# Seven block products for the up projection in half of each MLP

## The chip, the cores and the metric

The kernel runs on one core of one Trainium2 chip. The metric is the device time of one execution in microseconds: before the change the median of three runs is 1108.54, from 1107.82 to 1109.71.

TensorE (PE in the profile) multiplies matrices into PSUM, VectorE (DVE), ScalarE (ACT) and GpSimd (POOL) work on elements, SyncE (SP) issues transfers. Each engine runs its own instructions strictly in the order written for it and waits for the others by semaphores.

## The reference, cut to what matters

A two-layer encoder steps over 512 prompt tokens and 64 sampled ones, all in float32, 1024 wide. Layer 0 mixes tokens by causal pooling, layer 1 by sparse attention (an indexer picks keys, then grouped attention with rotary). Each layer ends with an MLP of hidden width 4096, and a last norm closes the step:

```
def _mlp(h, w_up, w_down):
    u = jax.nn.relu(h @ w_up)
    return (u * u) @ w_down

x = x + y                                        # y: the mixer's output
x = x + _mlp(_rmsnorm(x, norm_mlp[i]), mlp_w_up[i], mlp_w_down[i])
```

The change is in the two MLPs alone: 576 tokens x 1024 x 4096, up and down, in each layer.

## The kernel before

**Precision.** A float32 operand is held as two reduced parts: a high part wh or uh, made by a cast on ACT (L189, `wh`), and the rest wl or ul, made by a subtract on DVE (L190, `wl`). A product is three matmuls, wh by uh, wh by ul and wl by uh. A weight "unit" is 128x512 elements in both parts, and there are six plus two unit buffers in an MLP.

**Tokens and quarters.** The 576 tokens lie in columns, in two halves of 288. The hidden width is done in four quarters (c = 0 to 3) of 8 blocks of 128 rows. For each quarter, first up: a block takes two units and 48 matmuls (8 input tiles x 3 x 2 halves) into a double PSUM bank `up`, of which there are two. Then relu times the norm's scale on DVE (L385), the square on ACT (L386).

**Down by seven products.** Down takes rows and tokens in pairs. Over 2x2 blocks, b11 to b22 of activations, Strassen's scheme with Winograd's sums needs seven block products in place of eight. `factors` (L398 on) makes the operands: three blocks of the activations (L402 and L408, high and low part) and the four sums t1 to t4 (L403 to L406, then L407 and L409) into the tile u; the sums of weights come from two accumulating DMAs and two POOL adds (L231, L237). For each pair q of output blocks the three banks a, b and c take the products: b11 into a, t2 into b, t1 into c, then b21 into a, t3 into b, b22 into c, t4 into b, 84 matmuls in all. The first product b11 is needed in three outputs; it is collected over the quarters in a sum g on DVE (L476) and added to the residual x by three POOL operations at the last quarter (L481 to L483).

**The order.** A tile scheduler decides the order on each engine from priorities and free buffers before the program runs; the order is then fixed. In the program text, the first block of the next quarter's up stands ahead of each down, so that PE has work while the operands of down are made.

**Loads.** Weights come from memory in blocks of 128x1024; SP issues them into two plus two raw buffers. In the second layer's last quarter, two output blocks are left to the plain products of `last`, which also ends the kernel with the final norm; the tiles `rest` hold the block of activations that u lacks for it.

Of the kernel before, what the change touches and what calls it, by code (L numbers as in the profile page):

```python
# [43 lines left out]
UNITS = (6, 2)  # L44
# [3 lines left out]
RAWS = (2, 2)  # L48
MLP_BLOCKS = ("up", "even", "odd", "down")
LOADS_AHEAD = {True: 3, False: 1}  # L50
UP_ORDER = (0, 4, 1, 5, 2, 6, 3, 7)
FACTORS = ("b11", "b22", "b21", "t1", "t2", "t3", "t4")
# [3 lines left out]
def pool_dsa_kernel(ctx: ExitStack, tc: tile.TileContext, a, o):  # L56
# [5 lines left out]
    weights = ctx.enter_context(tc.tile_pool(name="weights", bufs=UNITS[0]))  # L62
# [73 lines left out]
    turns = {"raw": 0, "unit": 0, "spare": 0}  # L136

    def longer(what, sizes, mlp):

        if not (mlp and "more" in phase):  # L140
            return False
        t, turns[what] = turns[what], turns[what] + 1
        return t * sizes[1] // sum(sizes) != (t + 1) * sizes[1] // sum(sizes)

    def raw_tile(mlp=False):
        pool = phase["more"] if longer("raw", RAWS, mlp) else raws
        return pool.tile([P, 4 * 264], F32, tag="raw", name=uid("raw"))

    def load(src, n, queue, mlp=False):
        raw = raw_tile(mlp)  # L150
        queue.dma_start(raw[:, :n], src)
        return raw
# [3 lines left out]
    def mlp_jobs(layer, plain=0):  # L156
        for c in range(4):
            ups = [("up", a["w_up"][layer, c * 8 + f], KT * P) for f in UP_ORDER]
            jobs.extend(ups[1:] if c else ups)
            if c < 3:  # L160
                jobs.append(("up", a["w_up"][layer, (c + 1) * 8 + UP_ORDER[0]], KT * P))
# [14 lines left out]
    def unit(n=512, mlp=False):  # L176

        pool = phase["more"] if longer("unit", UNITS, mlp) else weights
        return [pool.tile([P, 528], F32R, tag=t, name=uid(t))[:, :n] for t in ("wh", "wl")]
# [7 lines left out]
    def split_unit(src, mlp, spare=False):  # L187
        h, l = spare_unit() if spare else unit(src.shape[1], mlp)
        act.copy(h, src)  # L189
        how["sub"].tensor_tensor(l, src, f32(h), ALU.subtract)  # L190
        return h, l

    def loaded():

        waiting = []
        while jobs or waiting:
            while jobs and len(waiting) < LOADS_AHEAD["more" in phase]:
                kind, src, n = jobs.pop(0)
                mlp = kind in MLP_BLOCKS
                raw = load(src, n, nc.sync if mlp else act, mlp)[:, :n]  # L200
                sums = None
# [167 lines left out]
    def mlp(layer, gi, late=0, end=None):  # L369
# [5 lines left out]
        def pairs(c):  # L375

            return (KT - LAST if end and c == 3 else KT) // 2
# [1017 lines left out]
```

## Time and profile before

| what | value |
|---|---|
| median of three runs | 1108.54 us |
| the profiled execution | 1109.8 us |
| its span in the profile | 1108.0 us |
| PE busy | 1087.8 us, 98% of the span |
| DVE busy | 821.8 us, 74% |
| ACT busy | 540.2 us, 49% |
| POOL busy | 348.6 us, 31% |
| moved by DMA | 138.73 MB, 125 GB/s |

The profiled execution lies 1.3 us above the median, and 1.8 us of it lie outside its span. A row of the page names the line of the kernel, the engine, the operation, and the tiles it writes and reads. The rows that start with a time are single instructions, or runs of them in the chain of waits: start, length, engine, and in brackets how long the engine had been idle and which instruction ended the wait. The span starts with the pool mixer; the first MLP lies from about 41 to 428 us, attention from 428 to about 706, the second MLP then to about 1083.

### The profile page before, as it was taken

What the parts mean: (1) busy time and instruction counts of PE and PEld (TensorE: products, weight loads), DVE (VectorE), ACT (ScalarE), POOL (GpSimd) and SP (SyncE); (2) the same over time, 40 slices, a digit from 0 to 9 for tenths busy, and PEclk for the clock granted to TensorE, in tenths of its full rate; (3) what the DMA queues carried; (4) which work ended last, traced back from release to release, by engine and by line L of the source; (5) the groups of instructions that cost most, each with busy time, mean ns of one, the idle gap of its engine ahead of it and who ended that gap; (6) DMA issues with size and microseconds to landing.
All of it is one profiled execution on the core that took longest, in us unless ns stands there. A gap on an engine that the chain in (4) does not pass through costs nothing.

```text
span 1108.0 us, 21062 instructions
## 1 busy us (share of the span) xinstructions
PE 1087.8 (98%) x8222; PEld 1066.4 (96%) x8222; DVE 821.8 (74%) x1502; ACT 540.2 (49%) x969; POOL 348.6 (31%) x325
## 2 busy tenths in 40 slices
PE   9999999999999999999889999999999999999997
PEld 8999999999999999999888898999999999999996
DVE  7867856866786797779987944767756866786784
ACT  8545434434434545344367776545434434434542
POOL 3312201302221261227686893012211302231241
PEclk9999999999999999999988999999999999999999
DMA  6443543554364345457741444543543554355212
GB/s 220 138 105 77 161 134 82 118 162 115 87 161 130 90 115 174 120 158 186 200 110 49 136 138 143 166 106 77 161 134 79 123 161 115 86 162 131 68 42 86
DMA packets 60611, 138.73 MB, mean 125 GB/s; under 512 B 9969, under 2 KB 21536, under 8 KB 60512
## 3 DMA queue, kind: packets, MB, share of 16 engines
q1 hardware_dynamic: 46544, 103.50, 30.9%
q0 software_dynamic: 8928, 16.26, 9.4%
q10 hardware_dynamic: 5040, 17.63, 5.1%
q8 instruction: 65, 1.06, 0.4%
q14 instruction: 34, 0.28, 0.1%
HBM read 122.28 MB, written 10.89 MB: 120 GB/s over the span
## 4 chain that ended last, share of the span: by engine, by line
PE 82%; DVE 5%; DMA 4%; SPq 2%; POOL 2%; issue 2%; ACT 2%; ACTq 0%; DVEq 0%; POOLq 0%
PE up L277 37%; PE b L445 13%; PE c L445 8%; PE a L445 8%; PE wo L277 3%; PE sc L1092 2%; PE pj L277 2%; PE wa L277 2%; PE pt L1118 1%; PE pb L826 1%; DMA raw<-in_w_in 1%; PE dn L277 1%; PE o L1150 1%; PE o L1143 1%; SPq L1265 1%
## 5 line engine op out<-in xcount | busy, mean ns | idle before, releaser
L277 PE MATMUL up<-xs,wh 128*128 128x288 f32 x2048 | 356.7, 296 | 0.2
L189 ACT CAST wh<-raw 128x512 fp32r<-128x512 f32 (+1 forms) x316 | 194.4, 621 | 306.2 <-PE up L277 133.0
L277 PEld LDWEIGHTS up<-xs,wh 128*128 128x128 f32 x2048 | 300.3, 188 | 1.0 <-DVE v L385 0.6
L190 DVE TENSOR_TENSOR wl<-raw,wh 128x512 fp32r<-128x512 f32 (+1 forms) x292 | 236.4, 813 | 63.2 <-ACT wh L189 57.9
L277 PE MATMUL up<-xs,wl 128*128 128x288 f32 x1024 | 219.2, 295 | 0.0
L277 PEld LDWEIGHTS up<-xs,wl 128*128 128x128 f32 x1024 | 164.4, 188 | 0.1
L445 PE MATMUL b<-u,wh 128*128 128x288 f32 x744 | 150.6, 296 | 0.2 <-DVE x L490 0.2
L231 POOL TENSOR_TENSOR sum<-sum,raw 128x512 f32<-128x512 f32 x31 | 52.7, 1701 | 243.7 <-DMA raw<-in_w_down 196.4
L445 PEld LDWEIGHTS b<-u,wh 128*128 128x128 f32 x744 | 119.5, 188 | 0.6 <-DVE x L490 0.4
L445 PE MATMUL b<-u,wl 128*128 128x288 f32 x372 | 109.4, 296 | 0.0
L189 ACT CAST wh<-sum 128x512 fp32r<-128x512 f32 x93 | 56.9, 620 | 107.6 <-PE up L277 42.9
L445 PE MATMUL a<-u,wh 128*128 128x288 f32 x496 | 101.5, 295 | 0.0
L445 PE MATMUL c<-u,wh 128*128 128x288 f32 x496 | 100.8, 295 | 0.0
L385 DVE SCALAR_TENSOR_TENSOR v<-up,rbm 128x576 f32<-128x576 f32 x60 | 45.2, 756 | 67.8 <-PE up L277 63.1
L214 POOL DMA_DIRECT2D raw<-in_w_down x31 | 27.0, 871 | 186.2 <-DMA raw<-in_w_down 93.1
L190 DVE TENSOR_TENSOR wl<-sum,wh 128x512 fp32r<-128x512 f32 x93 | 78.6, 849 | 3.8 <-ACT wh L189 2.5
L445 PEld LDWEIGHTS a<-u,wh 128*128 128x128 f32 x496 | 79.9, 188 | 0.0
L445 PEld LDWEIGHTS c<-u,wh 128*128 128x128 f32 x496 | 79.6, 188 | 0.1
L445 PE MATMUL a<-u,wl 128*128 128x288 f32 x248 | 73.5, 296 | 0.1
L445 PE MATMUL c<-u,wl 128*128 128x288 f32 x248 | 73.3, 295 | 0.0
L445 PEld LDWEIGHTS b<-u,wl 128*128 128x128 f32 x372 | 69.9, 188 | 0.0
L213 POOL DMA_DIRECT2D sum<-in_w_down x31 | 28.1, 915 | 125.2 <-DVE wl L190 86.7
(256 smaller groups left out, 2015.5 us busy)
## 6 DMA issues: line engine op xcount, KB each, us to landing
raw<-in_w_up SPq DMA_DIRECT2D x64, 512.0 KB, 3.6
raw<-in_w_down SPq DMA_DIRECT2D x64, 512.0 KB, 3.6
raw<-in_w_o ACTq DMA_DIRECT2D x16, 512.0 KB, 3.9
sum<-in_w_down SPq DMA_DIRECT2D x31, 256.0 KB, 3.8
sum<-in_w_down POOLq DMA_DIRECT2D x31, 256.0 KB, 5.3
raw<-in_w_down POOLq DMA_DIRECT2D x31, 256.0 KB, 4.1
raw<-in_w_in ACTq DMA_DIRECT2D x15, 512.0 KB, 4.4
q<-st SPq DMA_DIRECT2D x32, 144.0 KB, 2.5
```

The source lines that it names most:

```text
L189: act.copy(h, src)
L190: how["sub"].tensor_tensor(l, src, f32(h), ALU.subtract)
L213: pool.dma_start(s1, odd[:, 512:], accum_op=ALU.add)
L214: pool.dma_start(raw[:, :512], even[:, :512], accum_op=ALU.add)
L231: pool.tensor_tensor(s2, s1, a11, ALU.add)
L277: pe.matmul(pt[h][:, :m] if isinstance(pt, tuple) else pt[:, h, :m], wt, xs[k][:, part, c:c + m], start=(k == 0 and i == 0), stop=(k == n ...
L385: dve.scalar_tensor_tensor(v, pt[:, :, :HT], 0.0, halves(norm.rb), ALU.max, ALU.mult)
L445: pe.matmul(bank[:, :HT], wt, ut, start=first and j == 0 and i == 0, stop=last and j == 3 and i == 2, skip_group_check=True)
L826: pe.matmul(pt[:, c0:c0 + rhs.shape[1]], lhs, rhs, start=n == 0, stop=n == len(steps) - 1)
L1092: pe.matmul(pt[:, hh, :nw], q[:, 2 * s + hh], ks[g][:, part, :nw], start=part == 0, stop=part == 1)
L1118: pe.transpose(pp[:, c:c + P], pr[:, hh, kt * P:(kt + 1) * P], ident)
L1143: pe.matmul(oc[:, 2 * s + hh], pT[:, c:c + P], V[:, kt, vs], start=kt == 0, stop=kt == i)
```

## The change

Quarters 0 and 1 of each MLP (`PLAIN_CHUNKS = 2`) keep the plain up projection. In quarters 2 and 3 up is done by the same seven products as down: `seven` serves both, with the class `Up` or `Down` for what is done with the banks. For up the operands are halves of the normed x: four blocks are views of the tiles xs, the sums t1, t2 and t4 are made in quarter 0 from x (`x_sums`, between blocks three to six, three DVE operations, one ACT cast and one DVE subtract for each of four tiles `xt`), and t3 by a change of xs in place at the end of quarter 1 (`x_difference`).

The order of products is another: b11 goes into bank b, and ACT copies bank b into bank a (L511). Then t1 into c, t2 on top of b, b21 on top of a, t3 onto b, b22 onto c, t4 onto b. So the first product reaches all three outputs in PSUM, and neither g nor the POOL operations at the end are left. In the first four such groups of an MLP one extra matmul writes bank a ahead of the copy (L510, `SEEDED`). No block of the next quarter stands ahead of down any more. The raw buffers and the loads are halves of a block, four plus three; six units serve everything, the buffers of sums are three in place of four.

```diff
-FACTORS = ("b11", "b22", "b21", "t1", "t2", "t3", "t4")
+PLAIN_CHUNKS = 2
+SEEDED = 4
+FACTORS = ("t3", "t1", "t2", "b11", "b22", "b21", "t4")
...
+        def x_sums(j):
+            t = x_sums_tile()
+            xt.append(t)
+            raw, first = rough[:, 3 * j:3 * j + 3], rough[:, 12 + j % 2]
+            gain, minus = gv[:, gi, j:j + 1], negative[:, half + j:half + j + 1]
+            act.activation(first, x[j][:, :HT], AF.Copy, scale=gain)
+            dve.scalar_tensor_tensor(raw[:, 0], x[j][:, HT:], gain, first, ALU.mult, ALU.subtract)
+            dve.scalar_tensor_tensor(raw[:, 1], x[half + j][:, :HT], minus, raw[:, 0], ALU.mult, ALU.subtract)
+            dve.scalar_tensor_tensor(raw[:, 2], x[half + j][:, HT:], minus, raw[:, 1], ALU.mult, ALU.subtract)
+            act.copy(t[:, :, 0], raw)
+            dve.tensor_tensor(t[:, :, 1], raw, f32(t[:, :, 0]), ALU.subtract)
...
+        def seven(operand, late, on):
+            b, a_, c = (psum1(t) for t in "bac")
+            on.banks = [t[:, :HT] for t in (a_, b, c)]
+            w = next_unit()
+            product(b, w, operand, "b11", rows, True)
+            tasks[0] += 1
+            if tasks[0] <= SEEDED:
+                pe.matmul(a_[:, :HT], w[0][:, :P], operand(0, "b11", 0), start=True, stop=True, skip_group_check=True)
+            act.copy(a_[:, :HT], b[:, :HT])
+            w1 = next_unit()
+            if late:
...
+            else:
+                product(c, w1, operand, "t1", rows, True)
+                on.c()
+                product(b, next_unit(), operand, "t2", rows)
+            on.b()
+            for bank, factor, then in ((a_, "b21", on.lo0), (b, "t3", on.hi1), (c, "b22", on.hi0), (b, "t4", on.lo1)):
+                product(bank, next_unit(), operand, factor, rows)
+                then()
...
+            def hi0(self):
+                v = self.v
+                dve.tensor_tensor(v[:, 0], self.banks[2], snap[:, 1], ALU.add)
+                self.relu(0, v[:, 0], ALU.max, 0)
+                if end and self.at[0] == 3:
+                    left_over(self.at[1], v[:, 0])
+                first_sum(v)
+                middle_sums(v)
+                parts_of(self.u, v, slice(0, 3))
+
+            def lo1(self):
+                v = self.v
+                self.relu(5, self.banks[1], ALU.min, 1)
+                last_sum(v)
+                parts_of(self.u, v, slice(5, 7))
...
-        steps = [s for c in range(4) for s in [(c, i) for i in range(c > 0, 8)] + ([(c + 1, 0)] if c < 3 else []) + [(c, None)]]
...
+            if c < PLAIN_CHUNKS:
...
+                    if c == 0 and 2 <= i < 6:
+                        x_sums(i - 2)
+                if c == PLAIN_CHUNKS - 1:
+                    snap = halves(tmp("snap", "s2", 1))
+                    for j in range(half):
+                        x_difference(j)
+            else:
+                for j in range(half):
+                    up = Up(c, j)
+                    seven(of_x, False, up)
+                    us.append(up.u)
+            for q in range(pairs(c)):
+                seven(of(us), q == 0, Down(q))
```

Three places of the order, where rows read: line, operation, tile written, tiles read, shape.

First, ACT in quarter 0 of the first MLP, around the up blocks six and seven (casts of weights `wh`, of sums of x `xt`, of operands of down `u`, and squares of `v`). Before:

```order
L189 CAST wh_182_1165<-raw_162_1018 128x512
L189 CAST wh_184_1169<-sum_181_1163 128x512
L386 ACTIVATE v_161_1015<-v_161_1015 128x576
L402 CAST u_169_1080<-v_161_1015 128x3x288
L189 CAST wh_189_1234<-sum_171_1091 128x512
L407 CAST u_169_1080<-t_168_1079 128x4x288
```

Now:

```order
L181 CAST wh_188_1152<-sum_162_924 128x512
L434 CAST xt_183_1137<-rough_126_686 128x3x288
L472 CAST u_154_901<-v_153_900 128x7x288
L455 ACTIVATE v_172_1053<-v_172_1053 128x2x288
L455 ACTIVATE v_172_1053<-v_172_1053 128x576
```

and DVE at the same place, now:

```order
L182 TENSOR_TENSOR wl_189_1153<-sum_162_924,wh_188_1152 128x512
L435 TENSOR_TENSOR xt_183_1137<-rough_126_686,xt_183_1137 128x3x288
L473 TENSOR_TENSOR u_154_901<-v_153_900,u_154_901 128x7x288
L463 SCALAR_TENSOR_TENSOR v_172_1053<-up_171_1004,rbm0_148_863 128x2x288
L463 SCALAR_TENSOR_TENSOR v_172_1053<-up_182_1080,rbm0_148_863 128x576
```

The casts of u were two of three and four pieces behind squares; now one of seven pieces stands behind a cast of xt, and the relu of bank up_171 stands behind its subtract.

Second, DVE where the third quarter goes from up to down. Before:

```order
L385 SCALAR_TENSOR_TENSOR v_469_3284<-up_478_3305,rbm0_140_841 128x576
L190 TENSOR_TENSOR wl_493_3435<-sum_473_3295,wh_492_3434 128x512
L404 TENSOR_TENSOR t_479_3356<-v_469_3284,t_479_3356 128x288
L405 TENSOR_TENSOR t_479_3356<-v_469_3284 128x288
L406 TENSOR_TENSOR t_479_3356<-v_469_3284,t_479_3356 128x288
L408 TENSOR_TENSOR u_480_3357<-v_469_3284,u_480_3357 128x3x288
L190 TENSOR_TENSOR wl_495_3439<-raw_462_3221,wh_494_3438 128x512
L409 TENSOR_TENSOR u_480_3357<-t_479_3356,u_480_3357 128x4x288
L385 SCALAR_TENSOR_TENSOR v_486_3423<-up_485_3374,rbm0_140_841 128x576
```

Now:

```order
L479 SCALAR_TENSOR_TENSOR v_523_3407<-v_523_3407 128x288
L480 TENSOR_TENSOR v_523_3407<-v_523_3407 128x288
L565 SCALAR_TENSOR_TENSOR v_523_3407<-b_525_3409,rbm0_148_863 128x288
L473 TENSOR_TENSOR u_524_3408<-v_523_3407,u_524_3408 128x2x288
L182 TENSOR_TENSOR wl_555_3585<-sum_537_3471,wh_554_3584 128x512
L473 TENSOR_TENSOR u_524_3408<-v_523_3407,u_524_3408 128x3x288
L483 SCALAR_TENSOR_TENSOR v_523_3407<-v_523_3407 128x288
L182 TENSOR_TENSOR wl_557_3589<-raw_515_3322,wh_556_3588 128x512
L473 TENSOR_TENSOR u_524_3408<-v_523_3407,u_524_3408 128x2x288
```

The parts of the last operands u_480 stood ahead of the next quarter's block up_485; those of u_524 stand behind the relu of bank b_525, the last product of up.

Third, PE at the same place. Before, the end of the next quarter's block, then down:

```order
L277 MATMUL up_485_3374<-xs_117_653,wh_466_3231 128x288 x4
L277 MATMUL up_485_3374<-xs_117_653,wl_467_3232 128x288 x2
L445 MATMUL a_487_3426<-u_431_2946,wh_474_3297 128x288 x2
L445 MATMUL a_487_3426<-u_431_2946,wl_475_3298 128x288
L445 MATMUL a_487_3426<-u_446_3079,wh_474_3297 128x288 x2
```

Now, the end of the last up group (t4 into b_525) with down's b11 around it:

```order
L496 MATMUL b_548_3562<-u_499_3253,wh_538_3473 128x288 x2
L496 MATMUL b_548_3562<-u_499_3253,wl_539_3474 128x288
L496 MATMUL b_525_3409<-xt_155_905,wh_533_3448 128x288 x2
L496 MATMUL b_525_3409<-xt_155_905,wl_534_3449 128x288
...
L496 MATMUL b_525_3409<-xt_183_1137,wl_534_3449 128x288
L496 MATMUL b_548_3562<-u_524_3408,wh_538_3473 128x288 x2
L496 MATMUL b_548_3562<-u_524_3408,wl_539_3474 128x288
L496 MATMUL c_550_3564<-u_449_2943,wh_541_3493 128x288 x2
```

Three of the four parts of down's first product moved ahead of t4; the fourth, of u_524, follows t4 at once.

More of the change, by code (lines that the diff above doesn't have):

```diff
@@ L43 @@
 HEADS = {"a": 512, "c": 1024, "d": 1024}
-UNITS = (6, 2)
+UNITS = 6
 UNDER = 64
@@ L134, in __getitem__, with raw_tile, load @@
             return self.t[k // 2][:, k % 2]
[L136 to L152, printed above, removed]
+    turns = {"spare": 0}
+    def raw_tile(pool=raws, n=2 * 264):
+        return pool.tile([P, n], F32, tag="raw", name=uid("raw"))
+    def load(src, n, queue):
+        halves = [raw_tile()[:, :n // 2] for _ in range(2)]
+        for i, raw in enumerate(halves):
+            queue.dma_start(raw, src[:, i * n // 2:(i + 1) * n // 2])
+        return halves
     jobs = []
@@ L369, in mlp, with x_sums_tile, room @@
     def mlp(layer, gi, late=0, end=None):
-        norm = Norm(f"m{layer}")
-        xs = split_x(gi, norm, lambda k: pair_slot("xs", "xs"), late)
-        part_sums = [None] * (KT // 2)
-        rest = [None] * 4
+        scratch = []
+        def x_sums_tile():
+            return phase["xt"].tile([P, 3, 2, HT], F32R, tag="xt", bufs=KT // 2, name=uid("xt"))
+        def room():
+            if not scratch:
+                t = f32(x_sums_tile())
+                scratch.extend(t[:, i].rearrange("p a t -> p (a t)") for i in range(3))
+            return scratch.pop(0)
@@ L440, in product, with tiles, parts_of, first_sum @@
-        def product(bank, w, us, factor, js, first, last):
+            square(v)
+        def tiles():
+            return (phase["acts"].tile([P, 7, HT], F32, tag="v", bufs=1, name=uid("v")),
+                    phase["u"].tile([P, 7, 2, HT], F32R, tag="u", bufs=4, name=uid("u")))
+        def parts_of(u, v, f):
+            act.copy(u[:, f, 0], v[:, f])
+            dve.tensor_tensor(u[:, f, 1], v[:, f], f32(u[:, f, 0]), ALU.subtract)
+        def first_sum(v):
+            dve.tensor_tensor(v[:, 1], v[:, 3], v[:, 0], ALU.subtract)
@@ L441, in product @@
             for j in js:
                 wh, wl = (t[:, j * P:(j + 1) * P] for t in w)
-                uh, ul = (us[j][:, FACTORS.index(factor), i] for i in range(2))
+                uh, ul = (operand(j, factor, part) for part in range(2))
                 for i, (wt, ut) in enumerate(((wh, uh), (wh, ul), (wl, uh))):
-                    pe.matmul(bank[:, :HT], wt, ut, start=first and j == 0 and i == 0, stop=last and j == 3 and i == 2,
+                    pe.matmul(bank[:, :HT], wt, ut, start=first and j == 0 and i == 0, stop=j == 3 and i == 2,
@@ L545, in last @@
+        if end:
+            rest = []
+            for j in range(half):
+                if j % 2 == 0:
+                    t = x_sums_tile()
+                rest.append(t[:, j % 2])
+                split(rest[j], parked[j // 2][:, j % 2, :HT])
+            b11, b22, b21 = ([u[:, FACTORS.index(f)] for u in us] for f in ("b11", "b22", "b21"))
+            end([rest + b22, b11 + b21])
     def last(parts):
```

348 lines of the change are left out of this document (185 added, 163 removed).

## The prediction

> **What bounds the kernel now.** I read the totals and the groups of the page first, then the chain, the stages, and single instructions.
>
> ```profile
> PE 1087.8 (98%) x8222; PEld 1066.4 (96%) x8222; DVE 821.8 (74%) x1502; ACT 540.2 (49%) x969; POOL 348.6 (31%) x325
> L277 PE MATMUL up<-xs,wh 128*128 128x288 f32 x2048 | 356.7, 296 | 0.2
> L277 PE MATMUL up<-xs,wl 128*128 128x288 f32 x1024 | 219.2, 295 | 0.0
> ```
>
> PE has work 98% of the span; the up projections of both layers are 2048 + 1024 = 3072 of its 8222 matmuls. The 295 ns of one is not its cost, since matmuls overlap. The cost is read from the chain of waits, in order of time, where runs of matmuls have a length and a count:
>
> ```profile
> 62.36 0.77 DVE v L385
> 63.13 0.04 issue
> 63.17 38.52 PE up L277 x288
> ...
> 205.31 1.59 PE b L445 x12
> ...
> 243.52 49.45 PE up L277 x372
> ```
>
> 49.45 / 372 = 0.1329 us for one matmul of 288 columns; a product of down (12 matmuls) takes 1.59 us, the same rate. An up block of 48 is 6.4 us. So from 63.17, where the fourth block of the first quarter starts, blocks end at about 69.6, 76.0 and 82.4.
>
> ```profile
> core 0: us, PE busy (x) PEld busy (x) DVE busy (x) ACT busy (x) POOL busy (x), PEclk, DMA share, GB/s
> 42.00:102.00 60.00, 59.92 (x447) 59.26 (x447) 42.47 (x69) 29.08 (x44) 8.87 (x7) 1.00 0.36 87
> 146.00:201.00 55.00, 55.00 (x416) 55.00 (x415) 34.39 (x50) 24.05 (x33) 9.58 (x8) 1.00 0.40 106
> 201.00:242.00 41.00, 41.00 (x311) 41.00 (x310) 33.64 (x54) 16.47 (x27) 9.47 (x8) 1.00 0.57 145
> 428.00:676.00 248.00, 238.38 (x1874) 223.50 (x1873) 194.20 (x499) 142.52 (x341) 150.98 (x148) 0.97 0.48 137
> 1083.00:1108.00 25.00, 17.41 (x130) 16.22 (x129) 11.04 (x32) 5.49 (x13) 3.12 (x4) 0.94 0.29 95
> ```
>
> These stages are the first quarter's up, the third quarter's up and down, attention, and the end. PE is full in every MLP stage. DVE is full to 34.39/55 = 63% in a plain up stage, but to 33.64/41 = 82% in a seven-product stage: seven products put more on DVE for less on PE. This is what the change does to up.
>
> **What the change removes.** In quarters three and four of both layers the up projection falls from 8 x 48 = 384 matmuls to 4 x 84 = 336. That is 48 x 4 = 192 fewer, at 0.1329 us: **-25.5 us**. PE is full there, so the whole of it is gain unless something else becomes late. The rest of the sum is what becomes late.
>
> **Seeds.** The first four seven-product groups of each MLP issue one more matmul (L510): 8 x 0.133 = **+1.1**. The copies of bank b into bank a (L511, ACT) lie beside three later products (t1, t2: 3.2 us) before b21 needs bank a; ACT is busy 16.47 of 41 us there. Nothing. The sums g that they replace (L476 on DVE, three POOL adds at the end) free time on engines with room; nothing either.
>
> **The first quarter.** The sums of x for the later quarters are made between blocks three to six. On ACT (first order listing) the cast of wh_188 waits for a unit that the sixth block still reads, until 82.4. Behind it on ACT stand a cast of an x sum and the 7x288 cast of u_154, on DVE the subtract of u_154, and behind that (DVE row `L463 ... up_171_1004`) the relu that frees the double bank into which the seventh block writes; there are two such banks, used in turn. PE waits for this chain. Its durations:
>
> ```profile
> 82.38 0.62 ACT L189 CAST wh<-sum 128x512 fp32r<-128x512 f32 x1 [2.62 <-PE up L277]
> ...
> 153.53 0.69 ACT L386 ACTIVATE v<-v 128x576 f32<-128x576 f32 x1 [0.43 <-DVE v L385]
> 154.25 0.92 ACT L402 CAST u<-v 128x864 fp32r<-128x864 f32 x1
> ...
> 156.19 1.16 ACT L407 CAST u<-t 128x1152 fp32r<-128x1152 f32 x1
> ```
>
> ```profile
> 152.73 0.76 DVE L385 SCALAR_TENSOR_TENSOR v<-up,rbm 128x576 f32<-128x576 f32 x1 [2.09 <-PE up L277]
> ...
> 154.62 0.45 DVE L405 TENSOR_TENSOR t<-v 128x288 f32<-128x288 f32 x1
> 154.99 0.45 DVE L406 TENSOR_TENSOR t<-v,t 128x288 f32<-128x288 f32 x1
> 155.36 1.05 DVE L408 TENSOR_TENSOR u<-v,u 128x864 fp32r<-128x864 f32 x1
> 156.33 0.68 DVE L190 TENSOR_TENSOR wl<-raw,wh 128x512 fp32r<-128x512 f32 x1
> ```
>
> ```profile
> 87.88 1.35 DVE L409 TENSOR_TENSOR u<-t,u 128x1152 fp32r<-128x1152 f32 x1
> 89.15 0.75 DVE L385 SCALAR_TENSOR_TENSOR v<-up,rbm 128x576 f32<-128x576 f32 x1
> ```
>
> From start to start DVE takes 0.37 us for 288 elements (154.62 to 154.99), 0.97 for 864 (155.36 to 156.33) and 1.27 for 1152 (87.88 to 89.15): 0.30 per further 288, so 0.67 for 576 and 2.17 for 2016. ACT needs 0.92 and 1.16, so 1.88 for 2016. The chain: 82.4 + 0.62 (wh_188) + 0.92 (x sum, 864) + 1.88 (u_154) + 2.17 (its subtract) + 0.76 (relu) = 88.8. PE meanwhile has 13 matmuls of down ahead of the seventh block, 1.7 us. The stall is 6.4 - 1.7 = 4.7 us: 6.5 if two POOL adds (0.9 each, below) delay DVE inside it, and 0 if the order of the engines bends so that the relu is done before, which a fixed order excludes. The second layer has the same order: **+9.3** for both. In the old order a cast and a square stand there, and each double bank is read out one block after it was filled.
>
> **From up to down.** Before, the first up block of the next quarter (6.4 us of PE) ran between the last finished up block and down; now nothing does. Down's first product is drawn into the last up group by the scheduler for three of its four factors (third listing), but its last part, and the next product after, read u_524's b11, whose subtract (second order listing, `L473` into u_524, 128x2x288) stands behind the relu of bank b (`L565 ... b_525`), which waits for the last matmul of t4. So PE waits a relu of 288 (0.45 by the 288 rows), the subtract of 576 (0.75) and handovers of about 0.05 to 0.1: 1.1 to 1.7. Four such places: **+5.2**. Before, the same relu had a block to hide behind. The second quarter hands over to down with a plain block's relu (0.76), square (0.69 for 576 elements, as ACT L386 below), two sums (0.74), a cast (0.62, by 512) and a subtract (0.68), 3.5 us, while down has 33 matmuls, 4.4 us, that do not need it: covered by 0.9. For slips there, and for the last group of each MLP, whose t4 follows t3 in the same bank after an update (0.45), **+1.0**, between 0 and 4 x 0.9.
>
> **DVE in the up groups.** One up group asks of DVE seven weight splits (0.60 from start to start, 208.28 to 208.88 below), ten operations of 288 (0.37), and part subtracts of 576, 864 and 576 (0.67, 0.97 and 0.67): 4.2 + 3.7 + 2.3 = 10.2 us, against 84 x 0.1329 = 11.2 us of PE. That would fit, but POOL's two adds for each group stop some of it:
>
> ```profile
> 202.72 0.45 DVE L478 TENSOR_TENSOR x<-x,c 128x288 f32<-128x288 f32 x1
> 203.09 1.64 DVE L190 TENSOR_TENSOR wl<-sum,wh 128x512 fp32r<-128x512 f32 x1
> 204.65 0.68 DVE L190 TENSOR_TENSOR wl<-raw,wh 128x512 fp32r<-128x512 f32 x1
> 205.25 0.44 DVE L476 TENSOR_TENSOR g<-g,a 128x288 f32<-128x288 f32 x1
> ...
> 208.28 0.68 DVE L190 TENSOR_TENSOR wl<-raw,wh 128x512 fp32r<-128x512 f32 x1
> 208.88 0.44 DVE L490 TENSOR_TENSOR x<-x,c 128x288 f32<-128x288 f32 x1
> ```
>
> ```profile
> 202.89 1.29 POOL L237 TENSOR_TENSOR sum<-sum,raw 128x512 f32<-128x512 f32 x1 [2.04 <-DVE wl L190]
> ```
>
> ```profile
> L190 DVE TENSOR_TENSOR wl<-raw,wh 128x512 fp32r<-128x512 f32 x18 | 16.0, 887 | 0.9
> L190 DVE TENSOR_TENSOR wl<-sum,wh 128x512 fp32r<-128x512 f32 x9 | 7.0, 793 | 0.2
> ```
>
> ```profile
> L237 POOL TENSOR_TENSOR sum<-sum,raw 128x512 f32<-128x512 f32 x3 | 4.5, 1502 | 2.0 <-DVE wl L190 2.0
> L231 POOL TENSOR_TENSOR sum<-sum,raw 128x512 f32<-128x512 f32 x2 | 3.0, 1479 | 3.1 <-DVE wl L190 3.1
> ```
>
> While POOL adds from 202.89 to 204.18, a split that takes 0.68 elsewhere takes 1.64; the updates of x that read PSUM keep their 0.45. In 201 to 242 the 27 splits took 23.0 us, 4.6 over 27 x 0.68, for five POOL adds: 0.9 us each. The Trainium skill, "GPSIMD Engine Reference", Specifications, says that GpSimd shares its SBUF interfaces with VectorE and contends with DVE instructions that have two SBUF inputs; the trace agrees, 1.64 against 0.68.
>
> With two adds a group costs DVE 10.2 + 1.8 = 12.0 us, 0.8 more than PE. DVE falls behind; what it owes is paid where PE waits for DVE in earnest, at the relu of bank b ahead of down. Of the last group's work 3.9 us stand behind that relu (three part subtracts 2.3, one operation of 288, two splits of 0.6): 48.0 - 3.9 = 44.1 us of DVE ahead of it against 44.6 of PE in a stage of four groups. That leaves no debt, if DVE never idles in between; it does where it waits for a square or a cast, by a few tenths each time. I take one group's excess, 0.9 a stage, between 0 and the whole 3.4: four stages, **+3.6**. Inside the stage a debt of that size is covered: splits are made up to five products (5 x 1.59 us) ahead of use. In down a group asks DVE for 4.2 + 6 x 0.37 = 6.4 us and two adds: room.
>
> **The clock.** In the stages where PE has idle time its granted clock is 0.97 and 0.94, elsewhere 1.00. The new stalls of the first quarter come in pieces (to the u_154 cast, to its subtract, to the relu) of 2.4, 1.8 and 0.3 us, by the chain above; were the clock 0.94 over such a stall's 25 us, as at the end, a layer would lose 1.5. I take **+0.8** for both, 0 to 3.0. The Trainium skill, "TensorE: Matmul & The Clock Gate", HAM oscillation, speaks against the change here: an idle gap of over about 3.4 us sends the array back to half clock for some microseconds, which I estimate by that page at 1.7 us lost each time; by it the term is 0 if the gaps stay in pieces and 3.4 if they join. No run here shows it yet in an MLP stage.
>
> **The sum.** -25.5 + 1.1 + 9.3 + 5.2 + 1.0 + 3.6 + 0.8 = -4.5 us. The profiled execution took 1109.8 (span 1108.0 and 1.8 around it), 1.3 over the median of 1108.54; 1109.8 - 4.5 = 1105.3, and on the basis of the median **1104.0**.
>
> **The rivals.**
>
> 1. *The stalls hide.* If DVE keeps up in the up groups and the chain of the first quarter is not on PE's path (the relu before the big subtract, or down's products long enough to cover it), the seeds and half of the transitions remain: -25.5 + 1.1 + 2.6 = -21.8, **1086.7**. For it: ACT and DVE are busy 29.08 and 42.47 of the 60 us there, so what holds PE up is order, not load. Against: that order is fixed, and each link's duration is measured.
>
> 2. *DVE bounds the up groups: slower.* The place is the third and fourth quarters' up, the mechanism the stretched splits above with more weight: an up group has eight DVE operations with two SBUF operands beside its seven splits, where a down group has the splits alone, so an add can stop DVE for its whole 1.5 us. Then a group is 10.2 + 2 x 1.5 = 13.2 us, a stage 52.8 - 3.9 = 48.9 against PE's 44.6: 4.3 of debt at the relu ahead of down, four times 17.2 in place of 3.6. 1104.0 + 13.6 = **1117.6**. It decides from a debt of 0.9 + 4.5 / 4 = 2.0 a stage on, which is 12.6 us a group; there the gain is gone. For it: DVE is at 82% in down already. Against: the excess measured is 0.9 an add, not 1.5.
>
> 3. *Loads come late.* Seven half blocks are held where four whole ones were, and the sums, made of two transfers in turn, have three buffers for four. If this costs PE 1 us in each of the 16 up groups, 1104 + 16 = **1120**. Against: PE is full in every MLP row above, with the DMA share at 0.36 to 0.57.
>
> **How the numbers follow.** My forecast (1098 to 1110) has 0.45, rival 1 and what lies toward it (1084 to 1098) 0.25, rival 2 with what lies toward it (1110 to 1122) 0.23, rival 3 0.07. What a measurement of this kernel can tell from no change is about 0.2%, 2.2 us: 1106.3 to 1110.8 is the same. Of my forecast's 0.45 some 0.27 lies below 1106.3, with 0.25 from rival 1: faster 0.52. 0.16 of the forecast and 0.01 of rival 2 lie within: same 0.17. The rest, 0.02 of the forecast, 0.22 and 0.07, is slower: 0.31. The range leaves out a third of rival 1's side and, above, rival 3 and the top of rival 2, about 0.1 each: 1088 to 1118; the forecast's own is 1098 to 1110.
>
> **What would show it.** In the changed profile: PE's idle time in the up stage of the first quarter, put down to DVE's relu of the up tile, near 4.7 us and twice; four waits of 1.1 to 1.7 us for the tile u ahead of down's second product; in a stage of up groups a DVE share of nine tenths or more and at its end about 1 us more of that wait; copies into bank a with nothing waiting; 1536 matmuls into tile up in place of 3072, at 0.133 us each. I am wrong if up groups take over 12.5 us each, if PE waits for weights (wl, DVE) all along, or if the first quarter shows no stall.

## The result and the profile after

The changed kernel takes 1120.24 us (median of 4 runs, 1118.69 to 1125.15) against 1109.12 for the kernel before on the same occasions: 1.0109 times as long, 95% interval 1.0075 to 1.0142. It is slower by 11 us. The forecast was 1104.0 with a range of 1088 to 1118.

The profiled execution (span 1116.8) has the matmuls that were promised and does not turn them into time. Page and list of waits of PE (us in total, times, longest) of the changed kernel:

```profile
PE 1070.4 (96%) x8038; PEld 1040.5 (93%) x8038; DVE 889.0 (80%) x1655; ACT 607.4 (54%) x1152; POOL 389.1 (35%) x363
...
L496 PE MATMUL b<-u,wh 128*128 128x288 f32 x992 | 205.0, 298 | 15.9 <-DVE u L473 7.9
```

```profile
PE b L496 <- DVE v L579: 8.2, 12, 1.1
PE b L496 <- DVE u L473: 7.9, 6, 2.0
PE b L496 <- ACT u L472: 5.8, 6, 1.7
PE b L496 <- DVE x L536: 2.0, 3, 1.4
```

PE issues 184 matmuls fewer and is busy 17 us less, while DVE is busy 67 us more. PE's four longest sums of waits are all for one bank, b, 18.1 of the 23.9 us for DVE and the rest for ACT: L579 is the add that reads bank b after t3, ahead of t4; L472 and L473 make the operands u of down. The wait rows fall short by some 0.16 us each, since a matmul's modelled end (295 ns behind its start) lies behind the start of the next (133 ns).

By stages, core 0, the columns being length, busy time and instructions of PE, weight loads, DVE, ACT and POOL, the granted clock, DMA share and GB/s. Before, the first quarter's up and the third quarter's up:

```profile
41.34:101.53 60.19, 60.11 (x450) 59.45 (x448) 42.85 (x69) 29.27 (x45) 9.46 (x8) 1.00 0.36 86
243.35:292.81 49.46, 49.46 (x375) 49.46 (x373) 32.55 (x47) 22.81 (x32) 9.18 (x7) 1.00 0.35 93
```

After, the first quarter's up, the third and fourth quarter's up, and the same of the second MLP:

```profile
41.58:103.41 61.83, 57.57 (x415) 56.02 (x414) 47.00 (x79) 31.22 (x49) 5.18 (x5) 0.97 0.28 72
...
246.16:293.20 47.04, 45.19 (x335) 44.02 (x334) 44.16 (x75) 32.51 (x64) 18.55 (x16) 1.00 0.66 156
...
339.42:387.31 47.89, 44.94 (x336) 44.02 (x334) 44.95 (x75) 32.35 (x64) 18.24 (x16) 1.00 0.64 154
...
706.58:768.72 62.14, 58.35 (x414) 56.76 (x412) 41.85 (x72) 28.56 (x43) 5.15 (x5) 0.95 0.31 84
909.96:957.44 47.48, 45.08 (x335) 44.15 (x334) 44.49 (x75) 32.34 (x64) 18.25 (x16) 1.00 0.66 158
1003.68:1052.10 48.42, 44.95 (x336) 44.01 (x334) 45.63 (x79) 35.20 (x72) 18.62 (x16) 1.00 0.66 159
```

A stage of up groups is 333 matmuls, 44.3 us at 0.1329. It takes 47.0 to 48.4, and DVE is busy 44 to 46 of them: 94%. The first quarter has PE idle and a clock below 1.00 in both layers.

If each stage's length is set against its count of matmuls at 0.1329 us, the difference of 8.7 us between the two spans (1116.8 and 1108.0, rounded) is made up like this, in us for both layers:

| place | forecast | profiled |
|---|---|---|
| 184 matmuls fewer (192 less 8 seeds) | -24.4 | -24.5 |
| first quarter's up: stall and half clock | +10.1 | +12.9 |
| third and fourth quarter's up: waits inside and at its end | +3.6 | +13.8 |
| down behind them: rest of the way in, half clock, updates | +5.2 | +8.4 |
| down of quarters one and two, up of quarter two | +1.0 | +2.8 |
| all outside the two MLPs | 0 | -4.8 |

### The profile page after: what moved, and what is told of

Read it like the earlier page. It is cut to its first block, busy times and chain, and to the rows that moved or that the text cites. A ratio compares the mean times of both kernels' runs of the same rounds, so it can differ in the third digit from the quotient of the medians.

```text
span 1116.8 us, 21753 instructions
## 1 busy us (share of the span) xinstructions
PE 1070.4 (96%) x8038; PEld 1040.5 (93%) x8038; DVE 889.0 (80%) x1655; ACT 607.4 (54%) x1152; POOL 389.1 (35%) x363
## 4 chain that ended last, share of the span: by engine, by line
PE 72%; DVE 17%; issue 4%; DMA 3%; ACT 1%; POOL 1%; SPq 0%; DVEq 0%; ACTq 0%; POOLq 0%
PE b L496 21%; PE up L305 17%; PE c L496 11%; PE a L496 5%; DVE wl L182 4%; PE pj L305 3%; DVE u L473 3%; PE wo L305 3%; PE wa L305 2%; PE sc L1219 2%; PE pt L1245 2%; DVE v L565 1%; PE v L1119 1%; DVE work L1172 1%; PE pb L953 1%
## 5 line engine op out<-in xcount | busy, mean ns | idle before, releaser
L496 PE MATMUL b<-u,wh 128*128 128x288 f32 x992 | 205.0, 298 | 15.9 <-DVE u L473 7.9
L305 PE MATMUL up<-xs,wh 128*128 128x288 f32 x1024 | 180.0, 298 | 1.0 <-DVE v L463 1.0
L305 PEld LDWEIGHTS up<-xs,wh 128*128 128x128 f32 x1024 | 151.4, 190 | 1.9 <-DVE v L463 1.5
L260 POOL TENSOR_TENSOR sum<-sum,raw 128x512 f32<-128x512 f32 x47 | 74.6, 1588 | 220.4 <-DMA raw<-in_w_down 127.6
L182 DVE TENSOR_TENSOR wl<-sum,wh 128x512 fp32r<-128x512 f32 x141 | 96.5, 685 | 25.5 <-ACT wh L181 22.1
L305 PE MATMUL up<-xs,wl 128*128 128x288 f32 x512 | 110.0, 296 | 0.0
L473 DVE TENSOR_TENSOR u<-v,u 128x576 fp32r<-128x576 f32 (+3 forms) x76 | 85.8, 1129 | 15.8 <-ACT u L472 15.3
L264 POOL TENSOR_TENSOR sum<-sum,raw 128x512 f32<-128x512 f32 x47 | 72.6, 1545 | 48.5 <-DVE wl L182 34.7
L305 PEld LDWEIGHTS up<-xs,wl 128*128 128x128 f32 x512 | 82.9, 190 | 0.0
L472 ACT CAST u<-v 128x576 fp32r<-128x576 f32 (+3 forms) x76 | 68.6, 902 | 24.3 <-DVE v L483 15.2
L455 ACT ACTIVATE v<-v 128x288 f32<-128x288 f32 (+1 forms) x96 | 49.9, 523 | 36.7 <-DVE v L565 21.7
L305 PE MATMUL pj<-xs,wh 128*128 128x288 f32 x352 | 62.0, 295 | 1.3 <-ACT xs L294 1.3
```

What stands on the lines that cost most here:

```text
L260: pool.tensor_tensor(s2, s1, a11, ALU.add)
L264: pool.tensor_tensor(s2, s2, a12, ALU.add)
L305: pe.matmul(pt[h][:, :m] if isinstance(pt, tuple) else pt[:, h, :m], wt, xs[k][:, part, c:c + m], start=(k == 0 and i == 0), stop=(k == n ...
L455: act.activation(v, v, AF.Square)
L472: act.copy(u[:, f, 0], v[:, f])
L473: dve.tensor_tensor(u[:, f, 1], v[:, f], f32(u[:, f, 0]), ALU.subtract)
```

## The experiments

All runs are compared with runs of the kernel before on the same chip (median 1110 to 1111 us); the ratio is to those. Where a run is set against the changed kernel, the difference is that of the two medians; the changed kernel ran beside a median of 1109.1, so by the ratios every run below stands 1 to 3.5 us better against it. The names of lines move by a few where an edit adds lines.

**The two halves of the change apart.**

```diff
-PLAIN_CHUNKS = 2
+PLAIN_CHUNKS = 4
```

with the sums of x gone and the leftover operand split where its block is finished.

> All four quarters keep the plain up projection, and the sums of x are gone; down has the new order of products with the copy of the first product within PSUM, the half-block loads and the six units of the changed kernel. It parts the two halves of the change. Theory (the loss lies in the up groups and in the sums of x): seeds 1.1 us, 0 to 0.9 us at each of eight ways from up to down, and if the 4.5 us that attention gained in the changed kernel come from its loads they show here too: 1105 to 1113 us. Rival (the new down costs by itself, by copies in PSUM or late loads): 1116 or more.

Measured: 1111.29 us, ratio 1.0019 (0.9996 to 1.0043). The new down, its copies in PSUM and the half loads cost nothing that these runs tell from zero (the interval reaches to 4.8 us), and gain nothing. In the profiled executions the two MLPs and the end take 1.6 us more than before, attention 2.4 less. The loss, but for that, belongs to the seven products of up and their sums of x. The first quarter's up, without sums:

```profile
41.53:95.81 54.28, 54.19 (x409) 53.54 (x407) 36.95 (x60) 25.29 (x41) 5.56 (x5) 1.00 0.32 82
```

**The sums of x.**

```diff
                         if i:
                             norm.stats()
+                            x_sums(0)
+                            x_sums(1)
                         continue
+                    if c == 0 and i == 2:
+                        x_sums(2)
...
-                    if c == 0 and 2 <= i < 6:
-                        x_sums(i - 2)
+                    if c == 0 and i == 2:
+                        x_sums(3)
```

> The changed kernel, with the sums of x made in blocks two and three of the first quarter, where DVE is idle for 12 of 18 us, in place of blocks three to six. Theory (the two stalls ahead of the seventh block, 4.1 us each, come of the queue of sums, casts and the 7x288 subtract, and the half clock that follows costs another 1.7 and 3.4): all of it goes, 1120.2 - 13 = 1107 us. Rival (DVE is overloaded in that quarter anyway, so the stall comes one block later): 1117 to 1121.

Measured: 1113.76 us, ratio 1.0029 (1.0015 to 1.0044), 6.5 us less than the changed kernel: half of the theory. First quarters of this run:

```profile
41.93:101.82 59.89, 56.08 (x409) 54.89 (x408) 46.51 (x79) 30.55 (x49) 5.56 (x5) 0.97 0.28 75
705.94:760.70 54.76, 54.26 (x407) 53.61 (x406) 41.90 (x72) 27.44 (x43) 5.55 (x5) 1.00 0.35 95
```

In the second layer the stall and the half clock are gone, 62.14 us to 54.76 (6 of the 397 matmuls of up and early down now lie in the next stage, 0.8 us). In the first layer DVE is still busy with the norm at that time, and the sums now delay it: PE waits 2.7 us for the norm's sums and 1.6 for the next relu.

**POOL's adds.**

```diff
-            s2 = phase["sums"].tile([P, 512], F32, tag="sum", name=uid("sum"))
-            pool.tensor_tensor(s2, s1, a11, ALU.add)
+            s2 = s1
...
-                if n == 3:
-                    pool.tensor_tensor(s2, s2, a12, ALU.add)
```

> The changed kernel with POOL's two adds for each seven-product group left out; the sum that they made is replaced by another tile, so the products with it have other values. Theory (t4 waits for an add on DVE that is late because splits are stretched while POOL adds): without them DVE needs 10.2 us for an up group of 11.2, the waits of t4 fall from 10.4 us to the 0.35 that t3 right ahead of t4 costs in any case, 16 times: 5 us less, and the waits of down for DVE's updates go, 2 more: 1112 to 1114 us. Rival (the waits come of t4 standing right behind t3 alone): 1118 to 1120.

Measured: 1103.50 us, ratio 0.9937 (0.9917 to 0.9957): 16.7 us less than the changed kernel, more than twice the theory's 7. The third and fourth quarter's up of this run:

```profile
245.36:289.81 44.45, 44.12 (x336) 43.88 (x334) 39.79 (x75) 31.87 (x64) 6.90 (x8) 1.00 0.68 166
335.90:380.37 44.47, 44.12 (x335) 43.89 (x333) 39.81 (x75) 31.87 (x64) 6.90 (x8) 1.00 0.70 165
```

The same 75 operations of DVE take 39.8 us in place of 44.2 and 45.0, the same 333 matmuls 44.45 in place of 47.0 and 47.9, and no wait of t4 is left in the list of waits. So the place of t4 behind t3 costs nothing by itself (the rival), and the four stages give 11.7 of the 15.5 us between the two profiled executions. The run leaves out two things at once: the stretch of DVE's operations, and the wait of ACT's casts for POOL's sums (15.6 us of ACT's idle time in the changed kernel). The rows show the first, on the engine that t4 waits for; what the second is worth was not parted from it.

**The order of the last products.**

```diff
+                if factor == "b22":
+                    with tc.issue_after(third):
+                        product(bank, next_unit(), operand, factor, rows)
```

where `third` is the last matmul of t3.

> The changed kernel with the order of PE held as the program text has it: t3, then b22, then t4, in place of b22, t3, t4. Theory (t4 waits for the add that reads bank b after t3; 1.6 us of b22 between them cover the add's 0.45 and up to 1.1 of lateness): the waits of t4 fall from 10.4 us to 0 to 2 us, 1110 to 1112 us. Rival (DVE is the bound of the up groups, 12 us against 11.2, so the debt is only paid later, at the way into down): 1117 to 1120.

Measured: 1127.59 us, ratio 1.0156 (1.0123 to 1.0189): 7 us slower than the changed kernel by the medians and 5 by the ratios, whose intervals overlap: that it gains nothing is sure, that it loses is not. The add that t4 waits for is line 585 here:

```profile
PE b L496 <- DVE u L473: 9.2, 6, 2.1
PE b L496 <- ACT u L472: 5.7, 4, 1.8
PE b L496 <- DVE v L585: 4.7, 4, 1.6
PE b L496 <- DVE wl L182: 2.1, 4, 0.7
```

The waits of t4 fall from 8.2 us to 4.7. But the operations behind them on DVE are no earlier: waits for u grow, waits for weight splits (wl) appear, and the third quarter's down loses 2 to 3 us more in each layer. The rival held, that the debt is only paid elsewhere. That the whole is slower neither had foreseen: of the 9.3 us between the two profiled executions 3.2 lie in the MLPs, 3.4 in attention and 2.1 behind the second MLP, which no edit touched. The clock accounts for the first two: PE ran at half clock for 10.2 us in the first MLP and 10.2 in attention, where the changed kernel's profile has 3.4 and 3.4, and at half clock the 6.8 us more lose 3.4 in each place.

**Early operands and the sums, two edits together and one alone.**

```diff
             def lo0(self):
                 self.relu(3, self.banks[0], ALU.max, 1)
+                parts_of(self.u, self.v, slice(3, 4))
...
-                parts_of(self.u, v, slice(3, 5))
+                parts_of(self.u, v, slice(4, 5))
...
+                            with tc.issue_after(norm.added.ins):
+                                x_sums(0)
+                                x_sums(1)
```

> The changed kernel with two edits. The sums of x are made in blocks two and three, but behind the last addition of the norm, which the sums had delayed in the first layer of the run before (2.7 us at the norm's sums, 1.6 at the next relu, and 1.7 of half clock stayed there). And in an up group the operand b11 is split as soon as it is squared, not together with b22 behind the relu of t4. Theory: against the run with the sums moved (1113.8) the first layer's 5.5 to 7 us go, and of the four ways from up to down (1.5, 1.5, 1.5 and 3.9, with 1.7 of half clock) some 4: 1101 to 1104 us. Rival (DVE has no room: the earlier split takes 0.4 us ahead of the add that t4 waits for, 16 times): 1107 to 1110.

Measured: 1117.00 us, ratio 1.0060 (1.0042 to 1.0078). Worse than the sums moved alone (1113.76), and beyond the rival.

```profile
41.55:103.68 62.13, 57.69 (x404) 56.13 (x402) 47.68 (x79) 30.76 (x49) 7.44 (x5) 0.92 0.27 72
710.76:765.56 54.80, 54.32 (x407) 53.66 (x406) 42.08 (x73) 27.67 (x43) 5.54 (x5) 1.00 0.36 96
```

In the first layer the sums now stand in the norm's chain behind its statistics, PE waits 3.3 us for the diagonal matrix, and the clock falls to 0.92 of the stage. In the second layer, where DVE was idle, the same placement is free.

> The changed kernel with the second of these edits alone: b11 is split as soon as it is squared. Theory (down waits for a split that is ready but queued behind the relu of t4): 1120.2 - 4 to - 6 = 1114 to 1116 us, the rows of down's b waiting for u on DVE gone. Rival (the split's 0.37 us move into the waits of t4): 1118 to 1123.

Measured: 1120.70 us, ratio 1.0093 (1.0074 to 1.0112): no gain over the changed kernel. The rival held: with DVE in debt an earlier operation makes others later.

**Both, without the adds.** The edits just shown, and POOL's adds left out.

> Both edits, and POOL's two adds of each group left out as in the run before, so that products have other values. If the losses of the change are the sums' queue (13 us), the way into down (about 4 of 10) and the splits stretched by POOL's adds (16.7 as measured), they add up: 1120.2 - 13 - 4 - 16.7 = 1086.5, 1084 to 1089 us. Rival (the edits free the same time twice, the debt of DVE being one): 1095 to 1100.

Measured: 1090.16 us, ratio 0.9818 (0.9799 to 0.9836). It is 1.2 us above the theory's range and far below the rival. That is 13.3 us below the run without adds, where the same two edits had given 3.2 with POOL adding. The ways into down, which alone gained nothing, are free here: the list of PE's waits has no row for u above 0.3 us, and it begins with the first layer's norm:

```profile
PE rb L332 <- DVE xt L342: 2.2, 1, 2.2
PE up L302 <- DVE v L460: 1.8, 2, 1.3
```

**One quarter.** Both edits, with `PLAIN_CHUNKS = 3`.

> Both edits, with seven products for up in the last quarter alone (three plain quarters). Theory: half of the 25.5 us is gained, and half of the 10.4 us of t4's waits and two of the four ways into down are paid: 1109 - 12.7 + 1.1 + 5.2 + 4 + 2 (down) - 3 (attention) = 1105 us, 1102 to 1108, within 3 us of two such quarters, since a quarter is worth little after its own costs. Rival (the waits grow with the number of groups in a row, so one quarter pays much less): 1098 to 1101.

Measured: 1117.44 us, ratio 1.0061 (1.0041 to 1.0082); 12 us above the theory, and the same as with two quarters (1117.00). 48 matmuls a layer save 6.4 us, and the last quarter's up alone loses 3.6 and 4.9 of them; the largest piece that the theory left out is the first layer's first quarter, 61.05 us at a clock of 0.94 against 54.28 without sums, which does not halve with the number of quarters. The rest of the 12 us was not traced.

```profile
41.64:102.69 61.05, 56.62 (x403) 55.61 (x402) 47.69 (x79) 30.75 (x49) 7.46 (x5) 0.94 0.27 73
```

**The adds on DVE.**

```diff
-            pool.tensor_tensor(s2, s1, a11, ALU.add)
+            dve.tensor_tensor(s2, s1, a11, ALU.add)
...
-                    pool.tensor_tensor(s2, s2, a12, ALU.add)
+                    dve.tensor_tensor(s2, s2, a12, ALU.add)
```

> The changed kernel with the two adds of each group made by DVE itself in place of POOL, nothing left out. Without the adds the kernel took 1103.5. Theory (an add on POOL costs DVE more in stretched operations than the 0.6 us that it takes on DVE): an up group asks 10.2 + 1.2 = 11.4 us of DVE against 11.2 of PE, 44 groups of them in down have room: 1104 to 1109 us. Rival (an add at the head of DVE's queue waits for its transfer, and what stands behind it waits too; or any DVE work in an up group is paid in full): 1114 or more.

Measured: 1121.48 us, ratio 1.0093 (1.0075 to 1.0111): the rival's number, by the first of its two mechanisms. In the profiled execution the four stages of up groups do get shorter, 46.6 to 46.7 us each, 4.4 us in all. But once an add holds DVE for 5.0 us for its transfer; PE's waits for updates of x rise from 2.0 to 5.0 us, half clock takes 1.7 more in the MLPs, and attention 2.8. Then with b11 early, and the sums of x behind the norm's diagonal matrix:

> The adds on DVE, the sums of x made behind the diagonal matrix of the norm (two in block three and one behind each of blocks three and four, so that they delay neither the norm nor the seventh block), and b11 split as soon as it is squared. Nothing is left out. Theory: the three losses are apart, so this is the run without adds and with both edits (1090.2, in which the first layer's norm still lost some 7 us to the sums) less 7 plus what the adds take of DVE, 1 to 8 us: 1086 to 1093 us, which is faster than the kernel before. Rival (DVE's debt comes back with the adds' 1.2 us): 1098 to 1106.

Measured: 1109.71 us, ratio 0.9988 (0.9975 to 1.0001): 17 us above the theory's range and 4 above the rival's. Two things were left. In the first quarters the sums now cut into the chain of the first pair of blocks, from its relu at 62.96 to the end of its subtract at 78.0 by the timeline, and the next pair's relu, which needs its tile v, comes behind. And once, in the last quarter of the first MLP, the first add holds DVE for a transfer:

```profile
403.28 0.69 DVE L260 TENSOR_TENSOR sum<-sum,raw 128x512 f32<-128x512 f32 x1 [5.38 <-DMA sum<-in_w_down]
403.89 0.45 DVE L538 TENSOR_TENSOR x<-x,a 128x288 f32<-128x288 f32 x1
```

DVE is idle for 5.4 us, and the update that frees a bank stands behind; PE waits 4.1. With that add on POOL (the last run below) PE's longest wait for an update is 1.4.

**The sums in gaps, and where each add belongs.** One sum behind the norm's last addition, one behind the diagonal matrix, two behind the first pair of blocks:

```diff
+                            with tc.issue_after(norm.added.ins):
+                                x_sums(0)
...
+                    if c == 0 and i == 2:
+                        with tc.issue_after(marks[0].ins):
+                            x_sums(1)
...
-                    if c == 0 and 2 <= i < 6:
-                        x_sums(i - 2)
+                    if c == 0 and 2 <= i < 4:
+                        x_sums(i)
```

In the first of the two runs both adds are on DVE, the first of them behind the split of s1; in the second, only the second add is on DVE.

> As the run before (adds on DVE, b11 split early), nothing left out, but the sums of x are put into gaps of DVE: the first of four behind the norm's last addition, the second behind its diagonal matrix, two behind the first pair of blocks; and the first add of a group stands behind the split that waits for the same transfer, so that it can't hold DVE's queue by itself (5.4 us once in the run before, of which PE lost 4.1). Theory (the pair chain relu, square, sums, cast, subtract of 9.2 us per 12.8 us of PE must not be cut by the sums of x, since the next pair's relu waits for its tile v): first quarters lose 1 us each beyond the norm's 2.8 in place of 7, with no half clock there: 1109.7 - 12 - 4 = 1094, 1091 to 1098 us, faster than the kernel before by over 1%. Rival (the sums only move the delay): 1104 to 1110.

Measured: 1107.44 us, ratio 0.9962 (0.9947 to 0.9977). That is the rival's range. The 5.4 us are still 4.4: the scheduler put the add there again, ahead of an update. And PE still pauses for the next pair's relu, 3.3 us in the first layer and 2.9 in the second, with a stretch of half clock at both.

> The same placement of the sums and early b11, with the second add of each group on DVE and the first on POOL, as in the changed kernel. Theory (an add costs DVE more when POOL makes it, 16.7 us for 94 adds or so less about 0.2 us each where DVE is the bound): 2 to 5 us slower than with both on DVE, 1096 to 1100. Rival (the first add on DVE waits for its transfer at the head of the queue and costs as much): the same or faster, 1090 to 1094.

Measured: 1103.20 us, ratio 0.9935 (0.9917 to 0.9952). It leaves nothing out and is faster than both kernels: 7.2 us (0.65%) under the kernel before in its own comparison. The rival had the sign right. First quarter, third and fourth quarter's up:

```profile
42.46:99.58 57.12, 54.22 (x408) 53.57 (x407) 47.88 (x80) 30.50 (x49) 4.09 (x4) 1.00 0.30 78
241.30:287.10 45.80, 44.57 (x336) 44.10 (x335) 43.58 (x81) 31.97 (x66) 14.86 (x12) 1.00 0.67 159
332.70:378.52 45.82, 44.64 (x335) 44.17 (x334) 43.55 (x81) 31.97 (x66) 14.86 (x12) 1.00 0.68 161
```

The up groups lose 1.5 us a stage in place of 2.8 to 4.2, the first quarter 3.9 less than in the changed kernel, at full clock. That the second add is better on DVE is seen in the stages of up groups, which the placement of the sums does not touch. With b11 early and both adds on POOL the eight such stages of two runs took 48.2 to 49.7 us, as here:

```profile
247.84:296.41 48.57, 45.56 (x339) 44.59 (x338) 46.46 (x79) 32.49 (x68) 17.62 (x16) 1.00 0.63 153
```

With both adds on DVE, or the second alone, all twelve took 45.6 to 45.8 (half a us of the difference is 3 or 4 matmuls more). So an add whose operands have long landed was best on DVE. That the first, which waits for a transfer, is best on POOL is less sure: the last two runs differ by 4.2 us, but part of that is the clock. The run with both adds on DVE took from 1102.1 us in its execution with the highest mean clock (0.997) to 1110.8 in that with the lowest (0.986); at clocks of 0.992 and 0.993, which both runs have, the last run is 1.2 to 2.5 us faster.

## Why the prediction was wrong

**The gain** of 25.5 us and the **seeds** of 1.1 are there to the matmul.

**The first quarter** was right in size, and in its chain up to the subtract of u. The rows of the changed kernel follow the forecast link by link (ACT, then DVE, then the subtract as the chain of waits has it):

```profile
82.65 0.62 ACT L181 CAST wh<-sum 128x512 fp32r<-128x512 f32 x1 [1.30 <-PE up L305]
83.17 0.91 ACT L434 CAST xt<-rough 128x864 fp32r<-128x864 f32 x1
83.99 1.87 ACT L472 CAST u<-v 128x2016 fp32r<-128x2016 f32 x1
```

```profile
86.27 2.24 DVE L473 TENSOR_TENSOR u<-v,u 128x2016 fp32r<-128x2016 f32 x1
88.55 1.42 DVE L463 SCALAR_TENSOR_TENSOR v<-up,rbm 128x576 f32<-128x576 f32 x2
```

```profile
86.35 2.18 DVE u L473
```

The cast of wh begins at 82.65 (82.4 forecast); the 2016-element cast takes 1.87 (1.88) and the subtract 2.18 (2.17). PE's two pauses are 2.0 and 2.2 us, 4.1 in all with 4.7 forecast, and 4.1 in the second layer. But PE does not stop where the forecast had it, at the relu ahead of the seventh block:

```profile
85.91 0.40 PE L496 MATMUL b<-u,wh 128*128 128x288 f32 x1 [1.71 <-ACT u L472]
88.57 0.45 PE L496 MATMUL b<-u,wh 128*128 128x288 f32 x1 [2.00 <-DVE u L473]
89.54 0.73 PE L305 MATMUL up<-xs,wh 128*128 128x288 f32 x2
```

It stops at the matmuls of down themselves. Of the 13 that stand ahead of the block, counted as 1.7 us of cover, six run ahead of the stop and seven need u, its cast and then its subtract; when they are done, the relu is done too. Less cover and no wait for the relu (0.76) nearly cancel, so that the agreement of 4.1 with 4.7 is in part luck.

**The clock** was the first term that was missed: +0.8 forecast. After those two pauses PE's granted clock falls:

```profile
82.00:86.00 4.00, 2.24 (x14) 1.61 (x12) 4.00 (x7) 3.21 (x3) 0.86 (x1) 1.00 0.50 86
86.00:90.00 4.00, 2.00 (x9) 1.73 (x10) 3.94 (x4) 0.60 (x1) 0.86 (x1) 0.85 0.34 111
90.00:94.00 4.00, 4.00 (x25) 4.00 (x24) 1.73 (x5) 2.65 (x4) 0.00 (x0) 0.72 0.50 70
```

0.15 and 0.28 of 4 us are 1.7 us lost; in the second layer's first quarter 0.95 of 62.14 loses 3.1; at the last way into down another 1.6 go:

```profile
1054.00:1058.00 4.00, 3.49 (x15) 3.49 (x16) 3.43 (x6) 1.52 (x3) 0.00 (x0) 0.59 0.07 8
```

That is over 6 us, above the upper bound of 3.0 that the end of the kernel before had given. The argument that the stalls come in pieces of 2.4 and 1.8 us, and so cost little, was the error. The Trainium skill, "TensorE: Matmul & The Clock Gate", HAM oscillation, names gaps of over about 3.4 us; here pauses of 2.0 and 2.2 within 5 us were enough, so the measurement decides. The 1.7 us that I estimated by that page for one fall agree with the 1.7 measured.

**The up groups** were the step that failed most: "I take one group's excess, 0.9 a stage, between 0 and the whole 3.4", +3.6 in all, with 13.8 measured: 10.4 in waits of t4 and 3.0 in the first wait on the way into down. The place was wrong: DVE's debt is paid at t4 of each group, where PE waits for the add that reads bank b, and not only at the end of the stage. "Inside the stage a debt of that size is covered: splits are made up to five products ... ahead of use" holds for the splits, for which PE does not wait; t4 waits for an add that can't be made ahead, because it reads what t3 has just written, and the next group's first product (12 matmuls, 1.6 us), which PE does between t3 and t4, does not cover it. The wait of a t4 was priced for the last group of each MLP alone.

```profile
276.50 0.44 DVE L565 SCALAR_TENSOR_TENSOR v<-a,rbm 128x288 f32<-128x288 f32 x1
276.87 0.44 DVE L585 TENSOR_TENSOR v<-c,snap 128x288 f32<-128x288 f32 x1
277.24 1.29 DVE L182 TENSOR_TENSOR wl<-raw,wh 128x512 fp32r<-128x512 f32 x1
278.45 0.44 DVE L565 SCALAR_TENSOR_TENSOR v<-v,rbm 128x288 f32<-128x288 f32 x1
278.81 0.45 DVE L579 TENSOR_TENSOR v<-b,snap 128x288 f32<-128x288 f32 x1
```

```profile
276.67 1.29 POOL L264 TENSOR_TENSOR sum<-sum,raw 128x512 f32<-128x512 f32 x1
```

From 268 to 299 us DVE does not rest for half a microsecond; the split ahead of the add is stretched by the POOL add of 276.67. It starts 0.72 us before that add ends and takes 1.29 in place of 0.67, so that it loses 0.62, most of what was left of the add. The size was wrong because the credit of 3.9 us of work behind the last relu, which I set against the whole stage's debt, is of use only to a wait at its end. The 10.2 us of DVE for a group were right: without the adds four groups take 39.8 us. An add cost DVE less than the 0.9 us forecast (0.55, below), and still the stages lost nearly four times the 3.6. The second rival had the stage, the engine and nearly the sum: 1117.6, and I gave it 0.23. It too had the price wrong (1.5 us an add) and the place (the relu ahead of down), so that its nearness is in part luck. Its point of decision, 12.6 us a group, was too high: the groups ran at 11.8 to 12.1 us, and the gain was gone. And none of the three signs that I had named for being wrong came: no group took over 12.5 us, PE did not wait for weights, and the first quarter did stall.

**From up to down**, 1.1 to 1.7 us each was right three times (1.5). The fourth, in the last quarter of the second MLP, is 3.9 us and a half clock: ACT's copies of the leftover operand and casts of it stand among the casts that down waits for. These copies are in the program's text, and I didn't cost them. The four come to 8.5 us (3.0 of them are in the 13.8 above) with 5.2 forecast. The experiments add that splitting b11 earlier did not shorten these waits while POOL's adds stayed, and did without them.

**Outside the MLPs** I counted nothing. Attention, which is the same work, took 272.5 us in place of 277.0, its clock 0.99 in place of 0.97 (before, then after):

```profile
429.25:706.26 277.01, 267.39 (x2082) 251.98 (x2080) 213.11 (x532) 160.19 (x373) 152.77 (x150) 0.97 0.49 141
434.09:706.58 272.49, 263.46 (x2097) 248.41 (x2095) 218.46 (x538) 168.09 (x381) 152.89 (x150) 0.99 0.48 142
```

The clock alone can account for the gain: before, 17.1 us of attention ran at half clock, after 3.4, which is up to 6.8 us less lost. In the experiments attention took from 272.4 to 277.2, with 3.4 to 10.2 us at half clock, and the length does not follow these alone; what decides it, and how often the clock falls there, stays open.

**The third rival**, late loads, did not show: no wait of PE in the MLPs names a transfer. The range failed at its upper end by 2 us, because the bounds of two terms were drawn too close and the second rival's own upper end was left out.

## What to carry to other kernels

Fewer products of the same kind are paid with more elementwise work, so the stage to cost is the one where the second engine then has least room: an engine with work for 90% of the stage in strict order has no room for what stretches it, and its lateness is paid at the nearest tight reuse of a buffer, not at the end. Another engine's additions that stretch it belong in that sum in full, and moving one operation earlier on an engine in debt gained nothing here until the debt was gone. New preparatory work is put where that engine is idle in every layer that runs it; the same placement was free in one layer and cost 7 us in the other.

## What the runs showed of the hardware

Leaving out GpSimd's two adds of 128x512 for each group made the kernel 16.7 us shorter though they run beside everything: the same 75 DVE operations took 44.2 us with eight of them in the stretch and 39.8 without, 0.55 us an add.

The half clock came after pauses shorter than I expected, and in the changed kernel's MLPs for 3.4 us or 6.8. Two pauses of 2.0 and 2.2 us brought it there. In the run with the sums in gaps and both adds on DVE one pause of 3.3 did, and in the second layer one of 2.9:

```profile
726.00:730.00 4.00, 2.39 (x15) 1.94 (x13) 3.07 (x6) 2.86 (x6) 0.00 (x0) 1.00 0.17 66
730.00:734.00 4.00, 2.86 (x12) 2.87 (x13) 3.90 (x7) 2.14 (x3) 0.00 (x0) 0.56 0.13 42
```

In the last run one of 3.1 did not (the rows show 2.9 of it, since a matmul's modelled end is 0.16 us late):

```profile
62.00:66.00 4.00, 2.05 (x13) 1.61 (x11) 3.96 (x8) 2.82 (x5) 0.00 (x0) 1.00 0.20 66
66.00:70.00 4.00, 3.05 (x23) 3.05 (x24) 3.90 (x8) 2.18 (x4) 0.00 (x0) 1.00 0.02 4
```

So the length of a pause does not decide it alone; what does was not settled.
